# A hybrid decoder step on one core: operations set a stretch of work behind their loads, a sum of exponentials for each engine, and one chunk of the last head moved ahead

## The chip, the cores and the metric

The kernel runs on one core of a Trainium2 chip. The metric is the device time of one execution in microseconds (us); a shorter time is better. The core has five engines that run side by side, each in its own order: TensorE (PE in the profile; PEld is its loading of weights), VectorE (DVE), ScalarE (ACT), GpSimd (POOL) and SyncE (SP, which here only issues transfers). Transfers between memory and the core's buffers run on 16 DMA engines. An engine that meets an operation whose operand isn't there stands until it is, with everything behind it.

## The reference, cut to what matters

One layer is computed for a prompt of 2048 positions and for 8 decoded rows (one position each, with 512 cached positions in pages of 128):

```python
h = rms_norm(x, g_norm);  p = h @ w_in                  # 1024 -> 3592 columns
q, k, v, fz, za, u, gv, zc = split(p)
q, k = rms_norm per head;  logf = log_sigmoid(fz + b_f) # 8 heads of 64
c = cumsum(logf)
attn = softmax(q.k * SCALE + c_t - c_s, causal) @ v     # forgetting attention
mix  = tril(w_s) @ rms_norm(gv) + b_s                   # in chunks of 128 positions
y = x + concat(attn * silu(za), u * mix * silu(zc)) @ w_out
```

Outputs are y for prompt and decoded rows, and k, v, logf and the normalised gv.

## The kernel before, in words

All large products are made of two or three products of a high and a low part in a 32-bit format that TensorE takes in one pass; `split` (line 222) makes the parts: ACT, DVE or POOL writes the high part, DVE (L230) the rest. `split_weights` does the same with a factor.

There are three phases on TensorE.

Projections (lines 1083 to 1167): eight column groups of w_in, over 16 tiles of 128 positions for the first five groups, then over two of the four chunks of 512 positions for u, zc and za (`NCP = 2`; the other two chunks are left for later). After the first group, `gates` (497) makes log sigmoid and its running sum: `turn` transposes four blocks in a row on TensorE (L518, L160), ACT copies (L520), DVE scans (L521), and the split rows go to DRAM.

Attention (1170 to 1204): for each of 8 heads, `maxima` (842) computes the score products once to find each query's extreme (products into a `tp` bank, a DVE reduction at L861); `shifts` (868) turns four of them into rows by a TensorE transpose of `mx` (L876, L881) and sends them to DRAM. `values` (902) then computes for chunk c of 512 queries and key tile kt of 128 keys the scores (two products into one of two `sc` banks), the exponential on ACT (L926) into `p`, a sum of `p` into `acc` on POOL, every fourth on DVE (L933, L936), and, eight key tiles at a time, the products with the values (`av`). `add_up` and `done` transpose `acc` and send the reciprocal sums to DRAM (`rT`). `load_queries` (820) fetches the next chunk's queries and shifts three key tiles before the chunk ends. The maxima run 0.6 of a head ahead.

Filler: while attention runs, TensorE gets other products between its key tiles. `fill(ns)` (783) adds to a debt, which is paid in steps of three products (648 ns); `FILL` is the share of the attention's own time that is added. The generator `fillers` (775) gives first the 24 pieces of the projections that were left (12 column groups, two chunks each; `fill_weights` at 729 loads and splits 128 columns on POOL, L736 to L739), then loads w_out (`load_out_weights`, 992), then gives the output tiles.

Output (`out_tiles`, 1053): for each of 16 tiles of 128 positions `out_inputs` (1006) loads attention rows, gates, mixed rows and reciprocal sums (`az`, `m`, `r`), multiplies them on POOL and DVE (L1018, L1019) and splits them on ACT and DVE; `out_products` (1026) makes 48 products and adds x (L1038). What the attention phase leaves of this runs behind it.

The decoded rows run along: `decode_qk` and `decode_scores` during the projections, `decode_gate` at head 1 and `decode_attention` from head 2, `decode_out` and `out_sample` among the output tiles.

What sets the order: TensorE's instructions run as the program is written. The code keeps a clock of its own, `Pe.clock`, to which each product adds an expected time. `later(ns, fn)` puts `fn` off until that clock has moved on by `ns`, and `pump` runs what is due; `yield ns` in the decode generators does the same. The other engines' instructions and the DMA issues are ordered at build time by the Tile framework, from the order in the program, what is ready and which buffers are free. Buffers come from pools: 16 of 8 KB a partition (`s8`), 11 of 4 KB (`s4`), 3 for raw weights, `WK` of 2 KB (`s2`).

Of the kernel before, what the change touches and what calls it, by code (L numbers as in the profile page):

```python
# [36 lines left out]
FILL = 0.41  # L37
FILL7 = 0.42
LAG = 6400.0
AVB = 8  # L40
WK = 10
# [4 lines left out]
QCS = (0, 1, 2, 3)  # L46
DSUM = 4
# [4 lines left out]
DSTART = 2  # L52
OAHEAD = 2
# [17 lines left out]
def hymba_step(ctx, tc, x_prompt, x_sample, cache_k, cache_v, cache_logf, page_table, g_norm, w_in,  # L71
# [425 lines left out]
    def gates():  # L497
# [16 lines left out]
        def turn():  # L514
            for b in range(4):
                pt = bank("tp")
                for j in range(4):
                    transpose(pt[:NH, j * P:(j + 1) * P], lf3[:, 4 * b + j], ident)  # L518
                lT, cs = s2(t="lT")[:NH], s2(t="cs")[:NH]
                nc.scalar.copy(lT, pt[:NH])  # L520
                nc.vector.tensor_tensor_scan(cs, ones8, lT, 0.0 if b == 0 else last[:, b - 1:b],  # L521
                                             op0=ALU.mult, op1=ALU.add)
                nc.vector.tensor_copy(last[:, b:b + 1], cs[:, 511:512])
# [24 lines left out]
    def decode_gate():  # L548

        gvp = from_ps(OGV)  # L550
        gvn, _ = scaled(gvp, norm_factors(gvp, NG, P, rows=B), NG, P, rows=B)
        gvb = s2(t="gvb")[:B]
        nc.sync.dma_start(gvb, g_v[0].partition_broadcast(B))
        nc.vector.tensor_tensor(gvn, gvn, gvb, op=ALU.mult)
        nc.sync.dma_start(gvs_out, gvn)
        m2 = s2(t="m2")[:B]
# [4 lines left out]
        nc.vector.scalar_tensor_tensor(m2, m2, 0.5, from_ps(OU), op0=ALU.mult, op1=ALU.mult)  # L561
        nc.vector.tensor_tensor(m2, m2, silu2(from_ps(OZC)), op=ALU.mult)
        nc.sync.dma_start(am_s[:, 512:], m2)
        nc.sync.dma_start(z_s, silu2(from_ps(OZA)))
# [64 lines left out]
    def decode_attention():  # L629
# [5 lines left out]
        yield 5000  # L635
# [13 lines left out]
        own = small(8)[:BH]  # L649
        nc.sync.dma_start(own[:, 0:1], tiny[0].rearrange("b (h o) -> (b h) o", o=1))  # L650
        nc.sync.dma_start(own[:, 1:2], tiny[1].rearrange("b (h o) -> (b h) o", o=1))
# [3 lines left out]
        nc.vector.tensor_tensor(own[:, 2:3], own[:, 2:3], own[:, 0:1], op=ALU.min)  # L655
        nc.scalar.activation(lg, lg, AF.Exp, bias=own[:, 2:3], scale=-1.0, accum_out=own[:, 3:4])
        nc.scalar.activation(own[:, 4:5], own[:, 0:1], AF.Exp, bias=own[:, 2:3], scale=-1.0)
        nc.vector.tensor_tensor(own[:, 5:6], own[:, 3:4], own[:, 4:5], op=ALU.add)
# [26 lines left out]
    def decode_out():  # L685
# [6 lines left out]
        nc.vector.tensor_tensor(a2.rearrange("p (n d) -> p n d", n=NH),  # L692
                                from_ps(OV).rearrange("p (n d) -> p n d", n=NH),
                                prs.unsqueeze(2).to_broadcast([B, NH, HD]), op=ALU.mult)
        o4, ob, zb = s8(t="o4")[:B], s2(t="ob")[:B], s2(t="zb")[:B]
        nc.sync.dma_start(o4.rearrange("b (g n d) -> b g n d", g=NPG, n=NH),
                          o_s.rearrange("b g (n x) -> b g n x", n=NH)[:, :, :, :HD])
        nc.vector.tensor_reduce(ob, o4.rearrange("b (g f) -> b f g", g=NPG), axis=AX.X, op=ALU.add)
        nc.sync.dma_start(zb, z_s)
        nc.vector.tensor_tensor(a2, a2, ob, op=ALU.add)  # L700
        nc.vector.scalar_tensor_tensor(a2, a2, 0.5, zb, op0=ALU.mult, op1=ALU.mult)
        return am

    def out_sample(am):
# [7 lines left out]
        xys = s4(t="xys")[:B]  # L712
        nc.sync.dma_start(xys, xs)
# [15 lines left out]
    def fill_weights(o):  # L729
# [172 lines left out]
    def values(hd):  # L902

        h = hd["h"]
        for at, c in enumerate(QCS):
# [333 lines left out]
```

## Time and profile before

| | before |
|---|---|
| median of 3 runs | 1393.12 us (1387.74 to 1395.0) |
| the profiled execution | 1391.17 us, span 1389.5 us |
| TensorE busy | 1313.2 us, 95% of the span |
| VectorE, ScalarE, GpSimd busy | 704.3, 436.2, 548.6 us |
| TensorE's mean granted clock | 0.978 |
| moved by DMA | 174.71 MB, mean 126 GB/s |

The span runs from the first to the last instruction. Busy is the time in which at least one instruction of the engine ran; matmuls overlap and their ends are modelled, so a busy TensorE need not be at its peak. The granted clock is the share of full speed that TensorE was given; it is 1 or 0.5 at any moment. By the tile view the last filler product ran at 1180.8 us, and the output products follow it.

### The profile page before, as it was taken

Reading aid. Unit: us, or ns where it says so; the run is one execution under the profiler, and the core shown is the slowest. Engines: PE = TensorE matmul, PEld = TensorE weight load, DVE = VectorE, ACT = ScalarE, POOL = GpSimd, SP = SyncE. Lnnn points to the kernel's source line nnn. Section 1 sums busy time; section 2 is a strip of 40 time slices with the busy share of each in tenths; the row PEclk is TensorE's granted clock in tenths of the full one; section 3 lists DMA queues with packets and bytes.
Section 4 is the critical chain, followed back from the end, with each engine's and each line's share of the span. In section 5 each row is a group of like instructions: output and inputs, shape, how many; then the busy total and the mean of one; then the engine's idle time right before and its main releaser. Section 6 shows DMA issues by size and latency. Waiting matters only on the chain. (4 is left out here: it accounts for less than half of the span.)

```text
span 1389.5 us, 19601 instructions
## 1 busy us (share of the span) xinstructions
PE 1313.2 (95%) x6544; PEld 1012.4 (73%) x6544; DVE 704.3 (51%) x1376; ACT 436.2 (31%) x797; POOL 548.6 (39%) x647
## 2 busy tenths in 40 slices
PE   6998999999999999999998999999999959969998
PEld 5998999999887777766665665666656635748877
DVE  4446454535677544366655554555565663335131
ACT  5442222323122111034444443444444444211010
POOL 3113343323224555336654554646564444211010
PEclk9999999999999999999999999999999989989999
DMA  6553344545115565564325343455451253677521
GB/s 220 177 129 92 82 137 118 161 133 146 50 42 141 170 184 169 148 151 106 82 54 142 78 126 97 127 137 137 123 131 49 73 169 106 170 186 199 157 67 61
DMA packets 180791, 174.71 MB, mean 126 GB/s; under 512 B 39146, under 2 KB 141994, under 8 KB 179122
## 3 DMA queue, kind: packets, MB, share of 16 engines
q1 hardware_dynamic: 176802, 164.69, 44.3%
q10 hardware_dynamic: 3488, 8.39, 1.6%
q8 instruction: 52, 0.85, 0.3%
q14 instruction: 49, 0.40, 0.1%
q0 software_dynamic: 400, 0.38, 0.1%
HBM read 117.34 MB, written 56.08 MB: 125 GB/s over the span
## 5 line engine op out<-in xcount | busy, mean ns | idle before, releaser
L926 ACT ACTIVATE p<-sc,zero 128x512 f32<-128x512 f32 (+1 forms) x320 | 196.3, 623 | 186.1 <-PE sc L156 171.7
L936 POOL TENSOR_TENSOR acc<-acc,p 128x512 f32<-128x512 f32 (+2 forms) x176 | 202.5, 1150 | 130.5 <-ACT p L926 70.9
L861 DVE TENSOR_REDUCE mn<-tp 128x1 f32<-128x384 f32 (+6 forms) x320 | 189.5, 605 | 123.0 <-PE tp L156 120.5
L156 PE MATMUL acc<-wh,hh 128*128 128x384 f32 (+2 forms) x640 | 229.4, 358 | 0.4 <-ACT wh L235 0.4
L156 PE MATMUL acc<-wl,hh 128*128 128x384 f32 (+2 forms) x640 | 223.6, 349 | 1.2 <-DVE wl L238 1.2
L156 PE MATMUL acc<-wh,hl 128*128 128x384 f32 (+2 forms) x640 | 223.3, 349 | 0.6 <-DVE hl L230 0.6
L156 PE MATMUL sc<-q,k 128*128 128x512 f32 (+7 forms) x640 | 208.3, 402 | 5.5 <-ACT p L926 5.3
L156 PEld LDWEIGHTS sc<-q,k 128*128 128x128 f32 (+1 forms) x640 | 117.1, 197 | 28.0 <-ACT p L926 12.1
L156 PE MATMUL av<-p,vst 128*64 128x512 f32 (+3 forms) x640 | 135.9, 545 | 0.0
L156 PE MATMUL tp<-k,q 66*128 66x384 f32 (+6 forms) x320 | 124.2, 400 | 9.2 <-DVE mn L861 6.2
L156 PEld LDWEIGHTS acc<-wh,hh 128*128 128x128 f32 x640 | 121.4, 190 | 7.6 <-ACT wh L235 0.7
L156 PEld LDWEIGHTS acc<-wl,hh 128*128 128x128 f32 x640 | 121.4, 190 | 6.7 <-DVE wl L238 2.1
L156 PEld LDWEIGHTS acc<-wh,hl 128*128 128x128 f32 x640 | 121.0, 189 | 6.4 <-DVE hl L230 1.2
L218 POOL TENSOR_SCALAR sm<-sm 128x6 f32<-128x6 f32 (+3 forms) x84 | 20.9, 249 | 245.5 <-DVE sm L371 182.6
L156 PE MATMUL av<-wo,am 128*128 128x512 f32 x384 | 95.4, 407 | 10.8 <-DVE xy L1038 10.8
L156 PEld LDWEIGHTS av<-p,vst 128*64 128x64 f32 x640 | 47.9, 138 | 68.0 <-issue 59.3
L156 PEld LDWEIGHTS av<-wo,am 128*128 128x128 f32 x384 | 75.9, 198 | 28.0 <-DVE xy L1038 11.6
L156 PE MATMUL sc<-wo,am 128*128 128x512 f32 x384 | 90.6, 391 | 3.9 <-DVE xy L1038 2.8
L219 POOL TENSOR_TENSOR sm<-sm,mhalf 128x6 f32<-128x6 f32 (+3 forms) x84 | 89.0, 1060 | 6.7
L156 PEld LDWEIGHTS sc<-wo,am 128*128 128x128 f32 x384 | 71.8, 188 | 20.1 <-DVE xy L1038 3.3
L156 PEld LDWEIGHTS tp<-k,q 66*128 66x128 f32 x320 | 62.7, 196 | 32.3 <-DVE mn L861 8.9
L156 PE MATMUL fl<-hh,fh 128*128 128x512 f32 x192 | 81.7, 426 | 1.1 <-DVE sz L472 1.0
(209 smaller groups left out, 2021.9 us busy)
## 6 DMA issues: line engine op xcount, KB each, us to landing
raw<-in_w_in_dram SPq DMA_DIRECT2D x40, 256.0 KB
kb<-in_cache_k_dram SPq DMA_DIRECT2D x32, 256.0 KB
k<-qk_hi SPq DMA_DIRECT2D x16, 512.0 KB
q<-qk_hi SPq DMA_DIRECT2D x64, 128.0 KB
vb<-in_cache_v_dram SPq DMA_DIRECT2D x32, 256.0 KB
xy<-in_x_prompt_dram SPq DMA_DIRECT2D x16, 512.0 KB
out_dram<-xy ACTq DMA_DIRECT2D x15, 512.0 KB
xp<-in_x_prompt_dram SPq DMA_DIRECT2D x12, 512.0 KB
```

The lines of the kernel that those rows point to most:

```text
L156: nc.tensor.matmul(out, lhsT, rhs, start=start, stop=stop)
L218: nc.gpsimd.tensor_scalar(r, ss, inv_n, EPS, op0=ALU.mult, op1=ALU.add)
L219: nc.gpsimd.tensor_tensor(r, r, mhalf[:rows, :n], op=ALU.pow)
L861: nc.vector.tensor_reduce(part[:, i % 4, n:n + 1], sp, axis=AX.X, op=ALU.min)
L926: nc.scalar.activation(p[:, n0:], sp[:, n0:], AF.Exp, bias=zero1, scale=-1.0)
L936: eng.tensor_tensor(acc[:, n0:], acc[:, n0:], p[:, n0:], op=ALU.add)
```

## The change

- `gates`: the four blocks are no longer turned in one go; each block's split comes `GLAG` (2500 ns) after its transposes and then starts the next block.
- `shifts`: the transpose of the maxima comes 3000 ns behind them (`SLAG`) instead of 1500.
- `decode_gate` and `decode_attention`: loads first, then a `yield` of 6000 or 8000 ns, then the operations on them; both start at head 1 (`DSTART`), one behind the other.
- `fill_weights`: its two halves are split 7000 and 14000 ns behind their loads (`FLAG`); the filler waits for them. The first filler weights are loaded in the projection phase.
- `load_out_weights`: eight loads 1500 ns apart (`WOSTEP`), each split 7000 ns behind its load (`WOLAG`).
- `out_inputs`: loads m, z, a, r and now x, and the operations come 11000 ns later (`OLAG`); three tiles ahead instead of two (`OAHEAD`). `decode_out` is a generator with its loads ahead of its operations, and starts at tile 8 instead of 9.
- `values`: DVE sums every fourth exponential, and the one of key tile 2, into a tile of its own, `accd`; POOL sums the others into `acc`, the last diagonal one too, and adds `accd` to it once a chunk. `WK` grows by one for `accd`.
- The chunks of attention are one list, `UNITS`, in which (7, 0) stands ahead of (6, 3). `FILL` is 0.50 instead of 0.41, and 0.95 instead of 0.42 for the last three chunks.

```diff
-FILL = 0.41
-FILL7 = 0.42
+FILL = 0.50
+FILL7 = 0.95
+FLAG = 7000.0
+WOLAG = 7000.0
+WOSTEP = 1500.0
+OLAG = 11000.0
+SLAG = 3000.0
-WK = 10
+WK = 11
-QCS = (0, 1, 2, 3)
-DSUM = 4
+UNITS = [(h, c) for h in range(6) for c in range(4)] + [(6, 0), (6, 1), (6, 2), (7, 0), (6, 3), (7, 1), (7, 2), (7, 3)]
-DSTART = 2
-OAHEAD = 2
+DSTART = 1
+DGATE = 6000.0
+OAHEAD = 3
...
-        def turn():
-            for b in range(4):
...
+        def turn(b=0):
...
+            def parts():
                 ch, cl = s2(F32R, "ch")[:NH], s2(F32R, "cl")[:NH]
                 split(ch, cl, cs, "act")
                 for r, t in enumerate((ch, cl)):
                     nc.sync.dma_start(kx[:, r, b * 512:(b + 1) * 512], t.bitcast(F32))
+                if b < 3:
+                    turn(b + 1)
+            later(GLAG, parts)
...
     def decode_gate():
 
+        gvb = s2(t="gvb")[:B]
         gvp = from_ps(OGV)
-        gvn, _ = scaled(gvp, norm_factors(gvp, NG, P, rows=B), NG, P, rows=B)
-        gvb = s2(t="gvb")[:B]
         nc.sync.dma_start(gvb, g_v[0].partition_broadcast(B))
+        yield DGATE
+        r = norm_factors(gvp, NG, P, rows=B)
+        yield DGATE
+        gvn, _ = scaled(gvp, r, NG, P, rows=B)
...
+        u_, zc_ = from_ps(OU), from_ps(OZC)
...
+        yield DGATE
+        nc.vector.scalar_tensor_tensor(m2, m2, 0.5, u_, op0=ALU.mult, op1=ALU.mult)
...
+        za_ = from_ps(OZA)
+        yield DGATE
+        nc.sync.dma_start(z_s, silu2(za_))
...
-        yield 5000
+        own = small(8)[:BH]
+        nc.sync.dma_start(own[:, 0:1], tiny[0].rearrange("b (h o) -> (b h) o", o=1))
+        nc.sync.dma_start(own[:, 1:2], tiny[1].rearrange("b (h o) -> (b h) o", o=1))
+        yield 8000
...
+            got.extend((hi[:, k], lo[:, k]) for k in range(4 * half, 4 * half + 4))
+        for half in range(2):
+            raw = raw2().rearrange("p (k f) -> p k f", k=4)
+            nc.sync.dma_start(raw, w[half * 512:(half + 1) * 512, o:o + P].rearrange("(k p) f -> p k f", p=P))
+            later(FLAG * (1 + half), lambda half=half, raw=raw: halves(half, raw))
+        return got
...
-        later(1500, turn)
+        later(SLAG, turn)
...
+            if kt == 0 or kt == 2 and c:
+                p0 = p
+            elif kt == 1:
+                if n0:
+                    nc.gpsimd.memset(p[:, :n0], 0.0)
+                    n0 = 0
+                nc.gpsimd.tensor_tensor(acc, p0, p, op=ALU.add)
+            elif kt == 3 and c:
+                nc.vector.tensor_tensor(accd, p0, p, op=ALU.add)
+            elif kt % 4 == 3 and kt < 4 * c:
+                nc.vector.tensor_tensor(accd, accd, p, op=ALU.add)
+            else:
+                nc.gpsimd.tensor_tensor(acc[:, n0:], acc[:, n0:], p[:, n0:], op=ALU.add)
+                if kt == 4 * c + 1:
+                    nc.gpsimd.tensor_tensor(acc, acc, accd, op=ALU.add)
...
+            raw = raw2()
+            nc.sync.dma_start(raw, wo[k * P:(k + 1) * P, f * 512:(f + 1) * 512])
+
+            def parts():
+                split(hi, lo, raw, WOENG[n % len(WOENG)])
+                wo_hl[k, f] = hi, lo
+            later(WOLAG, parts)
+        for n, k in enumerate(KORDER):
+            later(n * WOSTEP, lambda n=n, k=k: load(n, k))
...
+        nc.sync.dma_start(xy, x[t0:t0 + P])
+        got = {}
+
+        def parts():
+            nc.gpsimd.tensor_tensor(z4, z4, r4, op=ALU.mult)
+            am = s8(F32R, "am")
+            hi, lo = (am[:, r * D:(r + 1) * D].rearrange("p (k t) -> p k t", k=KT) for r in range(2))
+            split(hi[:, 4:], lo[:, 4:], m4, "act")
+            nc.vector.scalar_tensor_tensor(a4, a4, 0.5, z4, op0=ALU.mult, op1=ALU.mult)
+            split(hi[:, :4], lo[:, :4], a4, "act")
+            got.update(hi=hi, lo=lo, xy=xy)
+        later(OLAG, parts)
+        return got
...
+            while i not in ins or not ins[i] or len(wo_hl) < 2 * KT:
                 prepare(i)
+                if last_phase[0]:
+                    Pe.waiting.pop(0)[2]()
+                else:
+                    yield -1
...
+                        fw = s8(F32R, "fw")
+                        first.append(fill_weights(OZA, (fw[:, :D], fw[:, D:])))
                         Pe.side = Pe.clock + SSTART
...
+    accd = s2(t="accd")
...
+    for at, (h, c) in enumerate(UNITS):
...
+        dose = FILL if at < len(UNITS) - 3 else FILL7
```

More of the change, by code (lines that the diff above doesn't have):

```diff
@@ L512, in step @@
                 later(3000, turn)
-        def turn():
-            for b in range(4):
[L516 to L523, printed above, removed]
+        def turn(b=0):
+            pt = bank("tp")
+            for j in range(4):
+                transpose(pt[:NH, j * P:(j + 1) * P], lf3[:, 4 * b + j], ident)
+            lT, cs = s2(t="lT")[:NH], s2(t="cs")[:NH]
+            nc.scalar.copy(lT, pt[:NH])
+            nc.vector.tensor_tensor_scan(cs, ones8, lT, 0.0 if b == 0 else last[:, b - 1:b],
+                                         op0=ALU.mult, op1=ALU.add)
+            nc.vector.tensor_copy(last[:, b:b + 1], cs[:, 511:512])
+            def parts():
                 ch, cl = s2(F32R, "ch")[:NH], s2(F32R, "cl")[:NH]
@@ L726, in out_sample, with fill_weights, halves @@
         nc.sync.dma_start(ys, xys)
-    def fill_weights(o):
-        hi, lo = (s4(F32R, t).rearrange("p (k f) -> p k f", k=KT) for t in ("fh", "fl"))
-        for half in range(2):
-            raw = raw2().rearrange("p (k f) -> p k f", k=4)
-            nc.sync.dma_start(raw, w[half * 512:(half + 1) * 512, o:o + P].rearrange("(k p) f -> p k f", p=P))
+    def fill_weights(o, pair=None):
+        hi, lo = (t.rearrange("p (k f) -> p k f", k=KT) for t in pair or (s4(F32R, "fh"), s4(F32R, "fl")))
+        got = []
+        def halves(half, raw):
             for k in range(4):
@@ L753, in filler @@
             unit = units.pop()
+            while len(unit) < KT:
+                yield -1
             for cp in range(NCP, 4):
@@ L762, in filler @@
                 yield 0
+        while min(len(unit) for unit in units) < KT:
+            yield -1
         for cp in range(NCP, 4):
@@ L992, in load_out_weights, with load @@
     def load_out_weights(f):
-        for n, k in enumerate(KORDER):
+        tiles = []
+        def load(n, k):
             if n % 2 == 0:
-                t = s8(F32R, "wo")
+                tiles.append(s8(F32R, "wo"))
+            t = tiles[-1]
             hi, lo = (t[:, (2 * (n % 2) + r) * 512:(2 * (n % 2) + r + 1) * 512] for r in range(2))
@@ L999, in load_out_weights @@
             nc.sync.dma_start(raw, wo[k * P:(k + 1) * P, f * 512:(f + 1) * 512])
-            split(hi, lo, raw, WOENG[n % len(WOENG)])
-            wo_hl[k, f] = hi, lo
+            def parts():
[4 more added lines that the diff above has]
+            later(n * WOSTEP, lambda n=n, k=k: load(n, k))
     def rows_of(t, t0):
@@ L1038, in out_products @@
             nc.vector.tensor_tensor(xy[:, fs], xy[:, fs], po, op=ALU.add)
+            yield 0
             if i == NT - 1:
@@ L1066, in out_tiles @@
                 pump(all_=True)
-                am = decode_out()
-            if i == 10:
-                gs = out_sample(am)
-                next(gs)
-            yield from out_products(i, *ins.pop(i), ("sc", "av") if last_phase[0] else ("fl", "fl"))
-            if i == 10:
+                gs = decode_out()
+            if gs is not None and i < 12:
                 next(gs, None)
+            yield from out_products(i, **ins.pop(i), tags=("sc", "av") if last_phase[0] else ("fl", "fl"))
     mgen = all_maxima()
@@ L1181, in hymba_step @@
         pump()
-    qload[0, QCS[0]] = load_queries(0, QCS[0])
-    for h in range(NH):
-        if h + 1 < NH:
+    qload[UNITS[0]] = load_queries(*UNITS[0])
+    vdone = 0.0
+    for at, (h, c) in enumerate(UNITS):
+        if c == 0 and h < NH - 1:
             heads[h + 1] = load_keys(h + 1)
-        vdone = 0.0
-        if h == DSTART - 1:
-            decode_gate()
-        if h == DSTART:
-            Pe.decode, Pe.steps = Pe.clock, decode_attention()
-        for c in values(heads[h]):
-            vdone += c
-            fill(c * (FILL if h < NH - 1 else FILL7))
+        if (h, c) == (DSTART, 0):
+            Pe.decode, Pe.steps = Pe.clock, chain(decode_gate(), decode_attention())
+        dose = FILL if at < len(UNITS) - 3 else FILL7
+        for v in values(at):
+            vdone += v
+            fill(v * dose)
             pump()
-            while mdone[0] / MT < min(h + vdone / VT + AHEAD, NH):
+            while mdone[0] / MT < min(vdone / VT + AHEAD, NH):
                 m = next(mgen, None)
```

179 lines of the change are left out of this document (76 added, 103 removed).

## The prediction

> **What bounds the kernel now.** I read the page's head first, then a table of stages (busy time and granted clock of each engine in stretches I cut at the visible gaps), then TensorE's waits, then the order of time around each gap.
>
> ```profile
> span 1389.5 us, 19601 instructions
> PE 1313.2 (95%) x6544; PEld 1012.4 (73%) x6544; DVE 704.3 (51%) x1376; ACT 436.2 (31%) x797; POOL 548.6 (39%) x647
> ```
> TensorE (PE) is the bound: 76.3 us idle in the whole span, and no other engine above 51%. So the change can gain only idle time of TensorE and the half clock that follows it. By stage (columns: stretch, its length, busy time of PE, its weight loads, DVE, ACT and POOL, then the granted clock, the DMA share and GB/s):
>
> ```profile
> 0.00:25.00 25.00, 13.98 (x72) 12.16 (x73) 13.06 (x25) 12.56 (x21) 9.39 (x25) 1.00 0.76 255
> 125.00:150.00 25.00, 21.00 (x115) 19.68 (x113) 16.06 (x29) 8.14 (x15) 6.28 (x8) 0.86 0.30 72
> 575.00:610.00 35.00, 33.04 (x145) 22.93 (x145) 22.16 (x42) 5.53 (x12) 15.02 (x27) 0.90 0.32 88
> 675.00:700.00 25.00, 22.82 (x99) 15.03 (x98) 18.11 (x31) 11.27 (x20) 13.18 (x18) 0.86 0.36 96
> 750.00:775.00 25.00, 19.75 (x90) 13.49 (x91) 13.21 (x29) 9.86 (x19) 6.08 (x6) 0.86 0.50 91
> 840.00:865.00 25.00, 23.06 (x102) 14.02 (x99) 10.83 (x23) 7.89 (x15) 9.28 (x11) 0.86 0.20 49
> 865.00:1115.00 250.00, 245.21 (x1234) 156.39 (x1234) 144.32 (x276) 113.59 (x204) 144.81 (x152) 1.00 0.42 112
> 1115.00:1150.00 35.00, 20.64 (x86) 11.53 (x86) 23.82 (x35) 16.17 (x30) 13.01 (x10) 0.85 0.55 164
> 1180.00:1260.00 80.00, 64.59 (x255) 51.29 (x256) 26.24 (x41) 13.57 (x23) 15.03 (x12) 0.89 0.77 190
> ```
> Idle is length less PE busy. The first stretch (11.0 us of start) is not touched by the change, nor is the end after 1260. Where the clock stands below 1.00, a part ran at half: 0.14 of 25 us is 3.5 us lost, beside the idle time. Seven stretches matter: 125 (4.0 idle + 3.5 clock), 575 (2.0 + 3.5), 675 (2.2 + 3.5), 750 (5.3 + 3.5), 840 (1.9 + 3.5), 1115 (14.4, and of 35 × 0.15 = 5.3 about half, since idle time lies in it: 2.6) and 1180 (15.4, and of 80 × 0.11 = 8.8 about 5.8). TensorE's waits (total, times, longest) say who is late:
>
> ```profile
> PE tp L160 <- DVE mx L876: 17.0, 9, 9.8
> PE av L156 <- DVE xy L1038: 10.8, 2, 6.2
> PE tp L156 <- DVE mn L861: 6.2, 3, 4.2
> PE sc L156 <- ACT p L926: 5.3, 6, 2.8
> PE tp L160 <- ACT lT L520: 4.0, 3, 2.0
> ```
> Nearly all name VectorE (DVE). Why it is late stands in the order of time (start, length, instruction, in brackets the idle time before and what ended it):
>
> ```profile
> 134.66 0.60 PE L160 MATMUL tp<-ident,lf 128*8 128x128 f32 x4 [1.77 <-ACT lT L520]
> 594.88 0.27 PE L160 MATMUL tp<-ident,mx 128*8 128x128 f32 x1 [1.26 <-DVE mx L876]
> 684.26 0.48 PE L156 MATMUL tp<-k,q 66*128 66x480 f32 x1 [1.66 <-DVE mn L861]
> 686.16 0.72 ACT L539 ACTIVATE th<-ps,zero 8x512 f32<-8x512 f32 x1 [2.77 <-DMA ps<-p_s]
> 760.28 0.15 DVE L652 TENSOR_TENSOR sm<-sm 64x1 f32<-64x1 f32 x1 [4.90 <-DMA sm<-tiny]
> 761.03 0.77 PE L156 MATMUL tp<-k,q 66*128 66x480 f32 x1 [4.16 <-DVE mn L861]
> 844.02 1.43 POOL L736 TENSOR_SCALAR raw<-raw,gT 128x128 f32<-128x128 f32 x4 [4.63 <-DMA raw<-in_w_in_dram]
> 846.18 1.35 DVE L936 TENSOR_TENSOR acc<-acc,p 128x128 f32<-128x128 f32 x1 [7.58 <-POOL acc L936]
> 848.88 0.30 PE L160 MATMUL tp<-ident,acc 128*128 128x128 f32 x1 [1.94 <-DVE mn L861]
> 1129.43 0.62 ACT L225 CAST wo<-raw 128x512 fp32r<-128x512 f32 x1 [5.23 <-DMA raw<-in_w_out_dram]
> 1144.75 0.38 PE L160 MATMUL tp<-ident,mx 128*8 128x128 f32 x1 [9.77 <-DVE mx L876]
> 1245.23 1.26 POOL L1018 TENSOR_TENSOR az<-az,r 128x512 f32<-128x512 f32 x1 [9.99 <-DMA m<-mT]
> 1249.24 0.80 PE L156 MATMUL av<-wo,am 128*128 128x512 f32 x1 [6.25 <-DVE xy L1038]
> ```
> One pattern: an engine stands at an operation whose load has not landed, and what TensorE needs is queued behind it. At 760 a 0.15 us DVE addition waits 4.90 us for a tiny load, and the maxima behind it hold PE for 4.16. At 844 POOL waits for a weight load, DVE waits for POOL's accumulator, PE for DVE.
>
> **The change, part by part**, each taken as a share of the loss above.
>
> *Gate rows (125).* The four blocks' transposes stood back to back; now 2.5 us of projection products lie between them on PE, and the copy and scan they wait for fit into that. Nothing is added. Takes 7.0 of 7.5.
>
> *Maxima shifts, 3000 instead of 1500 ns.* PE's transpose of mx comes 1.5 us later. Of the 17.0 us, 9.8 belong to stage 1115; the other eight waits are 7.2 us, 0.9 each, less than 1.5. With them goes the half clock at 575, where the first filler weights are also split earlier. I take 4.0 of 5.5 there and 4.5 of the other 6.0 (the one at 594.88 lies in 575). What is late next is the query load, which reads the shifts: it is issued three key tiles before its unit; for the moved chunk (7, 0) I followed the code's own bookkeeping of PE time, by which the load comes 8 us after the shift, so it is not late.
>
> *Decode gate (675).* Loads go out 6000 ns of PE work ahead, at four places. Takes 4.5 of 5.7. *Decode attention (750).* The tiny load goes 8000 ns ahead of the block instead of into its middle. Takes 8.0 of 8.8. Both begin one head earlier, with the same instructions.
>
> *An accumulator for each engine (840).* DVE's additions no longer wait for POOL's, only for the exponential; a merge on POOL is added.
>
> ```profile
> DVE acc L936 <- POOL acc L936: 58.3, 37, 7.6
> POOL acc L936 <- DVE acc L936: 32.9, 20, 7.4
> L936 POOL TENSOR_TENSOR acc<-acc,p 128x512 f32<-128x512 f32 x120 | 155.0, 1291 | 119.3 <-ACT p L926 62.8 <-DVE acc L936 32.9 <-DVE mn L861 5.4
> L936 POOL TENSOR_TENSOR acc<-acc,p 128x256 f32<-128x256 f32 x32 | 23.4, 731 | 2.8 <-ACT p L926 1.0
> L936 DVE TENSOR_TENSOR acc<-acc,p 128x512 f32<-128x512 f32 x48 | 34.3, 715 | 31.3 <-POOL acc L936 26.4 <-ACT p L926 4.6
> L936 DVE TENSOR_TENSOR acc<-acc,p 128x128 f32<-128x128 f32 x32 | 13.8, 431 | 32.2 <-POOL acc L936 31.8 <-ACT p L926 0.2
> ```
> POOL gives 24 additions (key tile 2) to DVE's sum and gains 24 merges, the same 1.29 us each; the 32 diagonal ones of 128 columns go from DVE (0.43) to POOL. That size is not in the trace on POOL: between nothing and 0.73 (256 columns), and the line from 1291 over 731 gives 0.45, which I take; so POOL +14 us over some 570, from 58% busy (144.8 of 250) to 61%, hidden by that room; without the room it would cost those 14 (23 at 0.73). DVE loses those 32 and the 58.3 us of standing. Takes 4.5 of 5.4: POOL may still wait for raw, but DVE no longer stands behind it.
>
> *Filler and output weights (1115).* A head is 17408 columns × 0.422 ns for the maxima (7.35 us) and four times that for the values (29.4). The filler's 24 pieces of 24 × 0.216 us are 124 us: at 0.41 that is 303 us of head work, more than the 294 there are, at 0.50 it is 249, so it ends in head 6 and the wo loads move from the last head to there. The 16 loads are spaced by 1500 ns, the splits put 7000 behind. But engines take operations in the order in which they become ready, not as the code stands:
>
> ```profile
> 1080.48 0.35 SPq L999 DMA_DIRECT2D raw<-in_w_out_dram  x1
> 1122.96 1.50 SPq L999 DMA_DIRECT2D raw<-in_w_out_dram  x3
> ```
> The first wo load went 40 us before the others, as soon as one of three raw buffers came free. So the lag binds TensorE's steps and what takes a new buffer in turn, and the splits perhaps not. Bounds 0 and 17.0; I take 8, the middle, since the tile inputs that shared the queue then (DMA 0.55) come later.
>
> *Output tiles (1180).* In this stretch 0.77 of the DMA engines' time is taken while several tiles' inputs arrive at once. Now three tiles ahead are asked for (two before), m first and x with them, and the first four can start before the longest unit of head 6, since (7, 0) goes ahead of (6, 3). Per tile the inputs are 1.5 MB; asked for some 30 us earlier they come at a lower rate. Same instructions; one more working buffer, which accd takes. Bounds 0 and 21.2; I take 13.
>
> *What is new.* Between the filler's end and the first tile PE has only values for about 19 us of its work (8 × 1500 + 7000), 20 key tiles. The exponential takes 0.69 us (below), PE's two score products 2 × 512 × 0.422 = 0.43 by the same bookkeeping, in runs of eight: 5.5 against 3.5, so 2.0 us late a run, or 0.6 with two banks (1.4) ahead; over two and a half runs 1.5 to 5. I take 3.5.
>
> ```profile
> L926 ACT ACTIVATE p<-sc,zero 128x512 f32<-128x512 f32 x224 | 152.5, 688 | 149.1 <-PE sc L156 138.9 <-POOL p L931 3.8 <-POOL acc L936 1.9
> ```
> Sum: 7.0 + 4.0 + 4.5 + 4.5 + 8.0 + 4.5 + 8 + 13 = 53.5, less 3.5: 50 us. The profiled execution took 1391.2 us (span 1389.5 and 1.7 around it), 1.9 under the median of 1393.1: 1341.2 in its terms, **1342** as forecast.
>
> **Rivals.**
> *A. The lags do nothing off TensorE.* For it: the load at 1080. Then only PE's own steps and the split accumulator count: 7.0 + 8.5 + 4.5, 6 of the decode (where new buffers hold the order), less 3.5: 22 us, 1369. Against it: the decode loads sat in the middle of their block in the trace, so their place does follow the code.
> *B. The last two stages stay bound by transfers.* 0.77 busy at 190 GB/s is near what the trace reaches at all (255 at the start). Then 8 and 13 go: 1363.
> *C. All of it goes.* 7.5 + 5.5 + 6.0 + 5.7 + 8.8 + 5.4 + 17.0 + 21.2 = 77, and nothing new: 1314.
> *D. The half clock stays.* It may not come from the short gaps, and three of the seven half clocks counted lie behind gaps of 1.3 to 1.9 us (575, 675, 840): 3.5 × 3 = 10.5 then remain, 1352. Against it, two finer stretches:
>
> ```profile
> 844.00:849.20 5.20, 3.26 (x16) 2.41 (x15) 3.02 (x4) 2.07 (x3) 4.63 (x7) 1.00 0.00 0
> 849.20:856.00 6.80, 6.80 (x23) 4.49 (x22) 4.29 (x13) 1.67 (x4) 1.63 (x2) 0.50 0.28 78
> ```
> Half clock for 6.8 us follows at once on 1.94 us of idle time. The Trainium skill, "TensorE: Matmul & The Clock Gate", What's actually happening, speaks for D: it asks for a whole idle window of about 3.4 us before the clock halves. The trace is against that rule at 849, where 3.26 of the 5.2 us before were busy.
> *E. Slower: POOL's merges.* Place: the merge at the second diagonal tile of 24 units, which waits for DVE's last sum, with two POOL additions and the transposes of acc behind it, these 5 us after the unit. If each merge waited as long as the longest such wait (7.4), PE would stand 2.4 us and lose 3.4 of clock each time: 24 × 5.8 = 139, and with the 50 gained 1480. It breaks even at 2.1 us a unit, 5 + 2.1 = 7.1 of wait without the clock. Against it: 32.9 us over 20 waits is 1.6 on average. The Trainium skill, "GPSIMD Engine Reference", 4.1 Engine selection, speaks for E: elementwise work belongs on VectorE, being about twice as slow on GpSimd; by the rows here 1291 stands against 715 ns.
> *F. No change:* the waits only change their names, each gap reappears before the next late operand; 1391.
>
> **How the numbers follow.** Chances: forecast 0.40, A and B together 0.25, C 0.14, D 0.07, E 0.07, F 0.07. The time is the forecast's. A and B (to 1369), C (1314) and D lie within 1312 to 1378, the ends a few us beyond them; outside are E and F. Half a per cent, about what a measurement here can tell, is 7 us: faster than 1386 are forecast, A, B, C and D, 0.86, and 0.01 of F; same 0.06; slower 0.07.
>
> **What would show it.** No wait of PE on lT, none over 1 us on mx; no clock of 0.5 near 135, 760 and 849; DVE's wait on POOL's acc from 58 us to under 15; fl products ending by 1100; PE's idle time from 76 to about 40 us. If DVE still waits for xy or wo loads as long, A or B is right; if tp<-ident,acc waits for POOL by tens of us, E.

## The result, and the profile after

The changed kernel took 1382.4 us (median of 12 runs, 1379.0 to 1389.8) against 1390.2 us of the kernel before beside it (12 runs, 1385.8 to 1398.4). The ratio is 0.9945, with a 95% interval from 0.992 to 0.997: 7.7 us faster. 50 us were forecast, and the range (1312 to 1378) does not hold the time. Its profiled execution took 1381.7 us.

The head of the page, after:

```profile
span 1379.9 us, 19555 instructions
...
PE 1311.9 (95%) x6544; PEld 1007.3 (73%) x6544; DVE 704.4 (51%) x1344; ACT 434.3 (31%) x797; POOL 572.0 (41%) x679
```

TensorE's idle time is 68.0 us (1379.9 less 1311.9), where it was 76.3 and about 40 had been forecast. To see where the time went I counted, in both traces, the work that TensorE has done by each moment (columns of each product, at least 256, at 0.422 ns), and compared the moments at which both kernels have done the same work. Negative is a lead of the changed kernel, in us:

```
work done    before at   changed
      120        152.3      -6.4
      600        684.3      -9.4
      720        837.9     -20.8
      760        890.8     -27.5
      880       1029.9     -27.1
      960       1126.2     -14.2
     1000       1190.0     -19.0
     1040       1252.0     -31.0
     1080       1295.5      -9.6
     1164       1384.7      -9.6
```

So up to 1003 us of its time the changed kernel is 27 us ahead, much as forecast; in the two last stages it gives 17.5 of them back. The stages of the kernel after (columns as in the prediction: stretch, length, busy time of PE, weight loads, DVE, ACT, POOL, granted clock, DMA share, GB/s):

```profile
120.00:145.00 25.00, 25.00 (x157) 24.20 (x156) 18.15 (x36) 10.05 (x19) 8.89 (x10) 1.00 0.36 87
...
665.00:690.00 25.00, 25.00 (x133) 17.16 (x130) 16.59 (x27) 11.96 (x23) 19.32 (x25) 1.00 0.53 142
...
1030.00:1100.00 70.00, 62.21 (x289) 39.24 (x288) 43.14 (x78) 31.15 (x59) 27.65 (x26) 0.93 0.39 109
1100.00:1150.00 50.00, 42.36 (x169) 24.11 (x167) 27.27 (x40) 23.20 (x43) 31.80 (x27) 0.79 0.43 118
...
1220.00:1290.00 70.00, 52.69 (x209) 41.59 (x208) 22.45 (x32) 5.99 (x10) 6.39 (x5) 0.90 0.57 156
```

The first two rows are the places at 125 and 675 of the prediction, shifted by the lead: full clock, and no idle time. The last three are where it is lost. The same last stretch before the change:

```profile
1220.00:1290.00 70.00, 59.22 (x236) 47.84 (x235) 26.40 (x35) 7.34 (x12) 7.68 (x6) 0.88 0.77 200
```

Before, TensorE did more there while more was moved (200 GB/s). Now TensorE stands 17.3 of 70 us with the DMA engines 0.57 busy. TensorE's waits of the kernel after, over the whole span (total, times, longest):

```profile
PE av L161 <- DVE xy L1081: 11.6, 4, 9.0
PE tp L165 <- DVE sm L989: 10.0, 4, 6.8
...
PE tp L161 <- ACT mt L914: 4.9, 2, 4.6
PE sc L161 <- ACT am L230: 4.8, 1, 4.8
...
PE tp L165 <- DVE mx L907: 2.3, 3, 1.3
```

Of the 17.0 us on mx 2.3 are left, and lT is gone. In their place stand waits on the sum of a row's exponentials (sm), on mt, on am, and still on xy. The longest, in order of time (start, length, instruction, idle time before and what ended it):

```profile
1250.78 0.34 ACTq L1086 DMA_DIRECT2D out_dram<-xy  x1
1250.80 5.78 PE L161 MATMUL av<-wo,am 128*128 128x512 f32 x24 [1.55 <-DVE xy L1081]
...
1257.83 5.74 PE L161 MATMUL sc<-wo,am 128*128 128x512 f32 x24 [1.25 <-DVE xy L1081]
1259.37 0.36 SPq L1057 DMA_DIRECT2D xy<-in_x_prompt_dram  x1
...
1261.11 0.55 SPq L1052 DMA_DIRECT2D az<-zT  x1
...
1269.94 1.26 POOL L1061 TENSOR_TENSOR az<-az,r 128x512 f32<-128x512 f32 x1 [20.52 <-DMA az<-zT]
1271.23 0.69 DVE L1065 SCALAR_TENSOR_TENSOR az<-az 128x512 f32<-128x512 f32 x1 [13.46 <-POOL az L1061]
1271.84 0.68 DVE L1081 TENSOR_TENSOR xy<-xy,av 128x512 f32<-128x512 f32 x1
...
1272.58 3.78 PE L161 MATMUL av<-wo,am 128*128 128x512 f32 x8 [9.01 <-DVE xy L1081]
```

Read it backwards. TensorE wants the bank `av` again. The 24 products that filled it ended at 1256.6, but VectorE adds them to xy only at 1271.84, because it stood 13.46 us at `az` of a later tile. That waited for POOL, POOL for a load of z, and the load of z was issued only at 1261.11: it lay in SyncE's queue behind a load of x, which got its buffer 8.6 us after the store of 1250.78 had been issued. SyncE's own waits between 1150 and 1300 us show that stand as the longest of its row:

```profile
SPq L1057 <- DMA out_dram<-xy: 12.4, 2, 9.9
```

TensorE did not lack its own operands; it waited for a sum queued behind somebody else's input. Two more such places, at the end of the filler and in the last chunks:

```profile
1095.40 0.62 ACT L230 CAST wo<-raw 128x512 fp32r<-128x512 f32 x1 [5.99 <-DMA raw<-in_w_out_dram]
...
1097.52 0.25 ACT L914 COPY mt<-tp 8x128 f32<-8x128 f32 x1
...
1097.82 0.71 PE L161 MATMUL tp<-k,q 66*128 66x416 f32 x1 [4.58 <-ACT mt L914]
...
1136.79 0.69 DVE L1065 SCALAR_TENSOR_TENSOR az<-az 128x512 f32<-128x512 f32 x1 [5.83 <-POOL az L1061]
...
1138.02 0.68 DVE L988 TENSOR_REDUCE sm<-tp 128x4 f32<-128x512 f32 x1
...
1139.59 1.26 POOL L1061 TENSOR_TENSOR az<-az,r 128x512 f32<-128x512 f32 x1 [2.83 <-issue]
...
1142.09 0.17 DVE L989 RECIPROCAL sm<-sm 128x4 f32<-128x4 f32 x1
1142.32 0.08 PEld L165 LDWEIGHTS tp<-ident,sm 128*4 128x4 f32 x1 [7.23 <-DVE sm L989]
```

At 1095 ScalarE stands 5.99 us at the split of an output weight, and the copy `mt` that frees a bank is behind it. At 1136.79 VectorE has stood 5.83 us at the inputs of a tile; it then works through the inputs of two tiles with POOL, and a reciprocal of 0.17 us, ready since 1138.7, comes last. VectorE's wait at a tile's inputs, before and after:

```profile
DVE az L1019 <- POOL az L1018: 38.0, 12, 6.1
```

```profile
DVE az L1065 <- POOL az L1061: 71.3, 13, 13.5
```

It nearly doubled. What the change put ahead is not only loads, but also the operations that stand for them.

### The profile page after: what moved, and what is told of

It is laid out like the page before. It is cut to its first block, busy times and chain, and to the rows that moved or that the text cites. A ratio compares the mean times of both kernels' runs of the same rounds, so it can differ in the third digit from the quotient of the medians.

```text
span 1379.9 us, 19555 instructions
## 1 busy us (share of the span) xinstructions
PE 1311.9 (95%) x6544; PEld 1007.3 (73%) x6544; DVE 704.4 (51%) x1344; ACT 434.3 (31%) x797; POOL 572.0 (41%) x679
## 5 line engine op out<-in xcount | busy, mean ns | idle before, releaser
L965 POOL TENSOR_TENSOR acc<-acc,p 128x512 f32<-128x512 f32 (+3 forms) x184 | 192.4, 1046 | 126.9 <-ACT p L952 116.6
L161 PE MATMUL av<-p,vst 128*64 128x512 f32 (+3 forms) x640 | 139.4, 556 | 0.2 <-ACT p L952 0.2
L161 PEld LDWEIGHTS sc<-q,k 128*128 128x128 f32 (+1 forms) x640 | 117.3, 198 | 29.4 <-ACT p L952 12.6
L161 PE MATMUL tp<-k,q 66*128 66x384 f32 (+6 forms) x320 | 120.7, 392 | 6.3 <-ACT mt L914 4.9
L161 PE MATMUL av<-wo,am 128*128 128x512 f32 x336 | 81.6, 400 | 11.6 <-DVE xy L1081 11.6
L161 PE MATMUL sc<-wo,am 128*128 128x512 f32 x336 | 80.4, 396 | 6.0 <-ACT am L230 4.8
L161 PEld LDWEIGHTS av<-wo,am 128*128 128x128 f32 x336 | 64.7, 194 | 27.0 <-DVE xy L1081 13.3
L161 PE MATMUL acc<-hh,wh 128*128 128x512 f32 x192 | 75.8, 395 | 4.2 <-DVE s L365 4.2
L161 PEld LDWEIGHTS sc<-wo,am 128*128 128x128 f32 x336 | 64.0, 191 | 20.4 <-ACT am L230 5.2
```

Source lines behind the costliest of these rows:

```text
L161: nc.tensor.matmul(out, lhsT, rhs, start=start, stop=stop)
L965: nc.gpsimd.tensor_tensor(acc[:, n0:], acc[:, n0:], p[:, n0:], op=ALU.add)
```

## The experiments

Each comparison ran the kernel before beside the others on the same chip (medians 1390.6 to 1392.8 us). "Saved" is one less the ratio, times 1391 us; the changed kernel saves 7.7 by this (4.2 to 11.1), and the interval of the others is 2.5 to 6 us to either side. Where two ratios are compared, "give or take" is the root of the sum of the squares of their half intervals.

### Which half of the change is at fault?

The theory: the early terms are real, and the new parts of the two last stages bring waits of their own. Rival: those stages are bound by transfers, and whatever comes earlier waits there. One run has the early parts alone:

```diff
-FILL = 0.50, FILL7 = 0.95, (7, 0) ahead of (6, 3)
+FILL = 0.41, FILL7 = 0.42, chunks in natural order
-load_out_weights, out_inputs, out_products, out_tiles, decode_out as changed
+the same functions as before the change
```

> Only the parts that work before 900 us: gate rows by turns, maxima shifts at 3000, the decode's loads ahead, an accumulator for each engine, the filler's first weights early. Filler share, order of the units, output weights and output tiles stand as before the change. Theory 1 (the early terms are real, and the new parts of the two last stages bring waits of their own that eat them): the lead of 27 us that the changed kernel has at 880 us of TensorE work stays to the end, 1390 - 27 = 1363, and DVE xy and mx waits of the last 300 us stay as before the change. Theory 2 (the last two stages are bound by their transfers, so whatever comes earlier waits there): 1380 to 1390.

The other has the late parts alone:

```diff
-SLAG, decode_gate, decode_attention, the sums in values, fill_weights as changed
+the same as before the change
 gates (turn, GLAG): as changed
```

> Only the late parts: filler share 0.50, order of the units, output weights spaced and put behind their loads, output tiles three ahead with x among their inputs, the sample rows at tile 8. Gate rows, shifts, decode, accumulator and the filler's first weights stand as before the change. Theory 1: the late parts cost what the changed kernel loses behind 880 us of work, 27.1 - 9.6 = 17.5 us: 1408, slower than before. Theory 2: the same as before within 5 us, 1385 to 1395. If it is faster than before by over 7 us, the late parts are not where the gain went, and the early terms are.

Measured: the early parts alone took 1374.3 us (ratio 0.9894, 0.985 to 0.9938; 14.7 saved), the late parts alone 1400.9 (1.0069, 1.0042 to 1.0095; 9.6 lost). All four expected times are missed (1363 and 1380 to 1390; 1408 and 1385 to 1395). e2 kept one early part, other than its expectation says: its gate rows are the changed ones, TensorE has no wait on lT and no idle time between 120 and 150 us there, and it leads by some 6 us at 120 us of work. So the late parts themselves cost more than the 9.6. The rival falls: with the filler's old share the early parts have a lead of 14.9 at 880 us of work, not 27, but all of it lasts to the end (14.7 saved), and the late half makes the kernel slower.

### Which late part?

```diff
 e3: the changed kernel with
-OAHEAD = 3; out_inputs, out_products, out_tiles, decode_out as changed
+OAHEAD = 2; the same as before the change
```

> The changed kernel with the output stage of before: inputs two tiles ahead in the old order and worked on where they are asked for, x loaded with the products, sample rows at tiles 9 and 10. Theory 1, narrowed to the output stage (SyncE's queue stands for buffers there, since x is held from the inputs on and the z and a loads lie behind it): the 21.4 us that the changed kernel loses between 1040 and 1080 us of its work come back but for the 6 that the stage lost before, 1382 - 15 = 1367. Rival (it is the early filler and output weights that cost, at 1040 to 1150 us): no change or slower, 1380 to 1395.

```diff
 e4: the changed kernel with
-FILL = 0.50, FILL7 = 0.95, (7, 0) ahead of (6, 3)
+FILL = 0.41, FILL7 = 0.42, chunks in natural order
```

> The changed kernel with the filler share of before (0.41, 0.42) and the units in natural order, so the filler ends in the last head again; output weights and output tiles as changed. Theory 1, narrowed to the output stage: its waits stay but come later, 1375 to 1385. Rival (the early end of the filler, values without filler and the moved chunk cost the 13 us lost between 920 and 960 us of work): 1382 - 13 = 1369 or less.

Measured: with the old output stage 1369.5 us (0.9852, 0.9812 to 0.9891; 20.6 saved, 12.9 more than the changed kernel, give or take 6.5). The last stretch in e3, to be read against the 52.69 us above:

```profile
1220.00:1290.00 70.00, 58.63 (x241) 46.82 (x240) 24.92 (x33) 6.04 (x11) 6.28 (x5) 0.90 0.60 168
```

With the old filler it took 1392.2 us (1.002, 0.9996 to 1.0043): 10.4 us worse than the changed kernel (give or take 4.8), a miss of both expectations. So the new output stage costs some 13 us, and the larger filler share, with the order of the units, is worth 10. It earns them elsewhere than expected: in e4 the lead at 880 us of work is 16.0, not 27.1, since at 697 and 747 us of time two waits (2.6 us on mx, 1.5 on acc) have a half clock behind them. The changed kernel has no such wait on mx, and full clock behind its own wait of 1.5 us on acc.

### What in the output stage?

Three of its steps were taken back one at a time, and once together:

```diff
 e5: x loaded, and its buffer taken, in out_products again, not in out_inputs
 e6: -OAHEAD = 3  +OAHEAD = 2
 e7: decode_out at tile 9, out_sample at tile 10, as before the change
 e9: e5, e6 and e7 together
```

> The changed kernel with one thing undone: x is loaded with a tile's products again, and takes its buffer there, not among the inputs. The old output stage as a whole won 12.9 us (1369.5). If x among the inputs is the cause (two of the eleven large buffers held per tile asked for, SyncE's queue standing for one with z and a loads behind it): at least 8 of these come back, 1374 or less, and the longest wait of TensorE on xy in the last stage (9.0) goes. If it is the third tile ahead or the sample rows at tile 8: 1378 to 1386.

> The changed kernel with inputs asked for two tiles ahead, not three; x still among them. If the number of large buffers in flight is the cause, from either end, this wins as much as x with the products: 1374 or less. If x's place alone decides: 1378 to 1386. If three ahead was worth something, as forecast: over 1386.

> The changed kernel with the sample rows' loads at tile 9 and their products at tile 10, in the old order of their operations. Theory of the buffers: one or two of the eleven large buffers (am, xys) are taken one tile later, a few us at most, 1378 to 1384. Rival (the sample rows, their 3.8 us reduction on VectorE and their loads ahead of the z loads cost the stage its 13 us): 1374 or less.

> The changed kernel with x loaded with the products, inputs two tiles ahead and the sample rows at tiles 9 and 10: the three single steps that won 8.4, 7.4 and 9.6 us, together. The lags and the order m, z, a of the loads stay. If the three relieve one shortage, they don't add: the old output stage as a whole won 12.9, 1369.5; the lags, worth 5.4 with three tiles ahead, may add to it: 1364 to 1370. If they are three causes of their own, they add to 25: 1357.

Measured: 1374.0, 1375.0, 1372.8 and together 1372.4 us (ratios 0.9868, 0.9890, 0.9847 and 0.9866). Each alone saves 7.6 to 13.6 us more than the changed kernel (give or take 5 to 6), and together they save no more. e5 came out at the edge of its theory, e7 as its rival had it, e6 between two expectations and e9 outside both of its own. Steps that don't add look like one cause, touched from three sides. A shortage of the eleven large buffers (az, xy, and two for the sample rows) would be such a cause, so one was taken away:

```diff
+            if i == 6:
+                held.append(s4(t="held")[:, :8])
+                nc.gpsimd.memset(held[0], 0.0)
...
+        if i == 13:
+            nc.vector.tensor_tensor(xy[:, :8], xy[:, :8], held[0], op=ALU.add)
```

> The changed kernel with one of its eleven large buffers taken away for the output stage: it is filled with zeros at tile 6, and eight of its columns are added to the sum of tile 13, one operation each. If the shortage is of these buffers, one less costs about what each of the three single steps won by giving back one or two: 7 to 10 us, 1389 to 1392. If it is the order of the loads in SyncE's queue or the transfers themselves, and not the number of buffers: the same within 4 us, 1378 to 1386.

Measured: 1374.7 us (0.9887, 0.985 to 0.9923). With a buffer less it is 8 us faster, not slower: the theory of the shortage falls, and the rival's 1378 to 1386 is missed as well. What all these steps change is the order in the engines' queues. The next four asked for bytes, stores and queue:

```diff
 e13: the load of x, and its addition, cut to 128 of 1024 columns (the rest of x is left out of y)
 e14: y stored in two halves, one behind each sum, not in one store
 e15: the same on e3
 e16: -nc.sync.dma_start(xy, x[t0:t0 + P])  +nc.scalar.dma_start(xy, x[t0:t0 + P])
```

> The changed kernel with only 128 of x's 1024 columns loaded and added per output tile (the other seven eighths of x are left out of y, their sums are copied instead). Same buffers held from the same points, same number of loads in the same queue, 7.2 MB less to move, some 38 us of transfers at 190 GB/s. If the last stage is bound by bytes (rival B of the prediction): the 21.4 us lost between 1040 and 1080 us of work shrink to a third, 1361 to 1370. If loads stand in SyncE's queue behind a load whose buffer is not yet stored: at most the stores' landing gets shorter, 1376 to 1384.

> The changed kernel with y stored in halves of 512 columns, the first one 5.2 us of products ahead of the second, in place of one store behind the second; same bytes. If loads stand for a buffer that a y store holds: the last half is 256 KB and lands earlier than 512 KB, each stand of SyncE on out_dram (30 us in 7 now) gets shorter, and 5 to 10 us come back, 1372 to 1377. If bytes bind: no change, 1379 to 1385.

> The changed kernel with the output stage of before (1369.5) and y stored in halves. If buffers held by stores still cost there (SyncE stands 24 us on out_dram in that run): 2 to 6 us, 1363 to 1367. If not: 1368 to 1371.

> The changed kernel with x's loads issued by ScalarE and not by SyncE: same buffers, same bytes, but z and a loads no longer stand behind an x load that has no buffer yet. If the order in SyncE's queue is the cause: the 9.0 us wait of TensorE near 1272 goes, and 8 to 13 us come back, 1369 to 1374, unless ScalarE then stands and the casts of a tile are late. If it is the number of buffers or the bytes: 1378 to 1390.

Measured: e13 1372.4 us (0.9867), between its two expectations. Its longest wait stays, at a low rate. A row of TensorE's waits between 1200 and 1300 us of e13, and the stretch around it:

```profile
PE av L161 <- DVE xy L1082: 7.7, 1, 7.7
```

```profile
1244.00:1260.00 16.00, 8.27 (x37) 6.52 (x35) 3.54 (x8) 1.27 (x3) 1.26 (x1) 0.86 0.35 91
```

With 0.35 of the DMA engines' time taken, full DMA engines don't explain that wait; how much of the 10.8 us that e13 gained is due to them can't be told from its changed order. e14 took 1387.8 us (0.9973): no gain, outside both expectations, and SyncE's waits for stores between 1150 and 1300 us didn't get shorter (32.0 us in 7, against 30.2 in 7); e15 1367.2 (0.9830, 0.9797 to 0.9863), at the edge of its own, and not told apart from e3. e16 took 1376.0 (0.9888, 0.9855 to 0.9922), 7.9 us better than the changed kernel (give or take 5.8) and between its two expectations; the wait of 9.0 us is gone, the longest on xy is 5.4. VectorE's wait for tile inputs between 1200 and 1300 us there, and, for comparison, in the changed kernel:

```profile
DVE az L1065 <- POOL az L1061: 27.9, 7, 6.5
```

```profile
DVE az L1065 <- POOL az L1061: 44.9, 7, 13.5
```

Over all runs, VectorE's longest wait at az in that stretch is 12.9 to 13.7 us in the kernels whose longest wait of TensorE on xy is 7.9 us or more (the changed one, e2, e4, e8, e11, e12, e14), and at most 10.8 in those with 6.2 or less, the kernel before among them. Two don't fit: e9 (6.8 and 8.7) and e10 (12.6 and 5.1). In e13 they are 12.5 and 7.7.

### The order on VectorE

```diff
+            else:          # from tile 4 on
+                nc.scalar.copy(hi[:, 4:], m4)
+                nc.gpsimd.tensor_tensor(lo[:, 4:], m4, hi[:, 4:].bitcast(F32), op=ALU.subtract)
+                nc.gpsimd.tensor_scalar(z4, z4, 0.5, 0.0, op0=ALU.mult, op1=ALU.add)
+                nc.gpsimd.tensor_tensor(a4, a4, z4, op=ALU.mult)
+                nc.scalar.copy(hi[:, :4], a4)
+                nc.gpsimd.tensor_tensor(lo[:, :4], a4, hi[:, :4].bitcast(F32), op=ALU.subtract)
```

> The changed kernel, but from tile 4 on the work on a tile's inputs is taken off VectorE: POOL multiplies (the factor 0.5 in an operation of its own, 128x512) and forms the two low parts, ScalarE casts as now; loads, buffers, queue order and bytes stay. Reading of the order of time near 1272: VectorE stands 13.5 us at a later tile's az, whose z load is late, and the sum xy<-xy,av, ready since 1256.6, is queued behind it; TensorE waits for that sum to free its bank, not for its own operands. If so, the waits of TensorE on xy (12.9 us in 5) fall to under 3 and their half clocks go with them: 1382 - 10 to - 16, 1366 to 1372. If TensorE lacks the operands themselves, the waits only change their name to ACT am or POOL am: 1378 to 1388.

> The same step on the best kernel so far (output stage of before, y in halves, 1367.2): from tile 4 on VectorE has only the sums xy. TensorE's waits on xy behind 1220 us, 9.0 us in 3, and some 5 us of half clock with them are at stake. Theory of VectorE's order: 1355 to 1362. If the operands themselves are late: 1364 to 1370, under the name ACT am or POOL am.

Measured: e17 1372.8 us (0.9862, 0.9825 to 0.9900), 11.5 us more saved than the changed kernel (give or take 6.3), though its loads, buffers and bytes are the same. Its median misses the expected stretch by 0.8 us, and the waits on xy are not under 3 us, as expected; but none on the operands came in their place. TensorE's waits on xy behind 1200 us fell from 12.9 us in 5 to the first row here; the second is VectorE's longest wait in that stretch:

```profile
PE sc L161 <- DVE xy L1089: 5.8, 1, 5.8
```

```profile
DVE am L718 <- POOL am L1074: 18.5, 1, 18.5
```

The one that is left has the same form: VectorE stands at the sample rows' first operation (L718), which was not moved, and four sums xy are queued behind it. e18 took 1364.1 us (0.9808, 0.9768 to 0.9848): the fastest here, some 27 us under the kernel before, but not told apart from e15, and at the edge of the rival's expectation. TensorE's waits between 1220 and 1300 us of e18:

```profile
PE sc L161 <- ACT am L1067: 8.9, 1, 8.9
PE sc L161 <- POOL am L1068: 2.6, 1, 2.6
```

No wait on xy is left, but two for the operands themselves are: in the old output stage VectorE's order hid that the inputs of a tile are late too. So two things hold that stage. In the changed kernel it is the order on VectorE: the waits on xy follow it, and fall by 7.1 us when the work is taken off. The time alone wouldn't show it, since e10, which only shuffled the order, saved nearly as much. Why e10's VectorE can stand as long and hold TensorE less is in its order of time:

```profile
1227.89 0.68 DVE L1081 TENSOR_TENSOR xy<-xy,sc 128x512 f32<-128x512 f32 x1
...
1229.27 0.68 DVE L1081 TENSOR_TENSOR xy<-xy,av 128x512 f32<-128x512 f32 x1
...
1243.19 0.69 DVE L1065 SCALAR_TENSOR_TENSOR az<-az 128x512 f32<-128x512 f32 x1 [12.64 <-POOL az L1061]
...
1246.62 0.79 PE L161 MATMUL sc<-wo,am 128*128 128x512 f32 x1 [5.10 <-DVE xy L1081]
```

Both sums had been made just before VectorE began to stand at 1230.55, so TensorE could fill both banks before it needed one freed, and waited 5.1 us. In the changed kernel the sum of one bank was still to come when the stand of 13.46 us began, and TensorE waited 9.0. So where a stand falls counts beside its length, and the changed kernel's loss is in part a matter of bad luck. Below VectorE's order lie late inputs, which come to light in e18. How the 12.9 us of e3 divide between the two stays open.

### The lags, and two early terms by themselves

```diff
 e8:  -OLAG = 11000.0, WOLAG = 7000.0   +OLAG = 0.0, WOLAG = 0.0
 e11: the sums of values as before the change (one accumulator)
 e12: decode_gate and decode_attention as before the change, one head later
```

> The changed kernel with both lags of the two last stages at nothing: the splits of the output weights and the work on a tile's inputs stand right behind their loads in the code. Rival A of the prediction (a lag does nothing off TensorE): the same within 4 us, 1378 to 1386, with the waits of ACT and POOL on their loads as long as now. If the lags do what they were meant for: slower by the 13 and more that the stages behind 1040 us lost before the change, 1392 or more.

> The changed kernel with the sum of exponentials as before: one accumulator for both engines, every fourth addition on VectorE. Forecast of its term: 4.5 us slower, 1387. By the leads (the changed kernel gains 6.7 us between 720 and 760 us of work, where the late parts alone gain 4.1) 3 to 7 us. Rival E (the merges on POOL cost time): faster, 1378 or less.

> The changed kernel with the decode's gate and attention as before: the loads in the middle of their blocks, one head later. Forecast of the two terms: 4.5 + 8.0 slower, 1395. By the leads between 600 and 720 us of work (the changed kernel gains 11.4 there, and the late parts alone lose 1.0) 12 us of lead, of which the stages behind 1040 us may take some: 1388 to 1395. If under 1386, the lead is lost there whatever it is.

Measured: without the lags 1387.8 us, between the two expectations. The kernel before took 1392.8 beside it, and the ratio, 0.9947 (0.9924 to 0.9969), is that of the changed kernel: the lags of 7 and 11 us are worth nothing that can be measured (0.3 us, give or take 4.7). One accumulator: 1388.2 (0.9984, 0.9952 to 1.0016), 5.4 us worse than the changed kernel, give or take 5.6, with 4.5 forecast: in the expected range, but not told apart from nothing. The old decode: 1398.2 (1.0058, 1.0035 to 1.0082), beyond the 1395 expected at most and 15.7 us worse, give or take 4.8, with 12.5 forecast.

## Why the prediction was wrong, point by point

**Gate rows** (7.0): the lead by 120 us of work is 6.4, and about 6 in e2, which has no other early part. Right. No wait on lT, and no half clock between 15 and 1039 us, so rival D is wrong as well.

**Maxima shifts** (4.0 and 4.5): between 120 and 600 us of work the lead grows by 3.0; between 760 and 880 it doesn't grow (27.5, 27.1). The long waits on mx went, but the second figure was a sum over waits that lie in the other terms' stages.

**Decode gate and attention** (4.5 and 8.0): the lead grows by 11.4 between 600 and 720, and e12 loses 15.7. Right in kind, but the size is not the decode's alone. Counted in the same way, the lead by 720 us of work is 20.8 in the changed kernel, but only 8 to 13 in e1 and e4 (old filler share), e11 (old sum) and e12 (old decode): without any one of the three, most of the growth is missing. (The prediction has both parts begin one head earlier; the gate began at head 1 before as well.)

**An accumulator for each engine** (4.5): e11 loses 5.4, give or take 5.6. The lead grows by 6.7 between 720 and 760, where this term was sought, but by at least as much in e11 without it; what e11 lacks, it lacks before 720. VectorE's wait on acc, 58.3 us before, is gone. Rival E is wrong: the merges took 31.8 us on POOL, as costed, with 1.4 us of idle time before them in all, and an addition of 128 columns took 0.49 us there (0.45 was taken). Both rows of POOL's groups, after:

```profile
L967 POOL TENSOR_TENSOR acc<-acc,accd 128x512 f32<-128x512 f32 x24 | 31.8, 1324 | 1.4
...
L965 POOL TENSOR_TENSOR acc<-acc,p 128x128 f32<-128x128 f32 x32 | 15.5, 486 | 3.1 <-ACT p L952 1.4
```

Together these terms seem to give 27.1 us of lead where 32.5 were forecast. That the two are so close is partly luck: the early parts alone (e1) have 14.9 there, and the rest comes only with the filler's larger share, which the prediction had put into a later stage.

**Filler and output weights** (8, less 3.5 of new cost): between 880 and 1000 us of work the lead falls by 8.1, where a gain of 4.5 was forecast. This is the first step that failed. The filler did end early (at 1091 us), and its share is worth 10.4 us (e4), but in the decode stretch; in its own place the splits of the output weights and the first tiles' inputs now stand in the queues of ScalarE and VectorE while the last chunks need these engines (the rows at 1095 and 1136 to 1142). The marks divide the loss only roughly, since the lead swings from row to row (14.2, 19.0, 31.0). Of the 17.5 us lost behind 880, e3 brings back 12.9, so some 4.6 are left for these parts; the wait at 1142 is not in e3, so it is a cost of the new output stage. No run took the splits away alone. The prediction also misread its row at 1080: it was the second of three early loads of w_out (1031.4, 1080.5, 1082.6), not the first and only one.

**Output tiles** (13, bounds 0 and 21.2): the lead falls by another 9.4, and e3 shows a cost of 12.9 (give or take 6.5) where 13 were to be won. This is the second step that failed, and the larger one. The prediction took the DMA share of 0.77 for the limit, and an earlier request for a cure. But the row it quoted, TensorE's wait on xy, has VectorE in it, and the pattern it had found at 760 and 844 (an engine stands at an operation whose load has not landed, and what TensorE needs is behind it) holds here too: asking for inputs earlier put more of such operations in front of the sums. Its lower bounds of 0 for both stages had no reason; a loss should have been in them.

**Rivals.** Of A (1369), the part on the lags of the last stages is borne out by e8: the sentence "the lag binds TensorE's steps ..., and the splits perhaps not" should have weighed more. Against A, the decode's loads ahead of their operations did their work (e12, which takes back yields and places together). B (1363) came to a time in which those stages give nothing; in fact they took 17.5 us, and not by transfers alone. That a gain in one place is given back in the next, which F held for all gaps, was true of the late half of the change only.

**Chances.** "Faster" held 0.87 and was right, by 7.7 us, hardly more than the 7 that the prediction had set for it; no case held both that the early terms come and that the late ones cost.

## What to carry to other kernels

Before an input is asked for earlier, look at which engine works on it and at what else is queued on that engine: on an engine that takes its instructions in order, an operation that waits for a load blocks the small sum or copy that frees TensorE's bank. A lag in a planner's clock for one engine need not move the operations of the others (e8); moving the waiting operation to an engine whose queue doesn't hold those sums takes the wait away (e17). A lead won early is worth only what the last stage can carry, so cost that stage with a loss among its bounds.

## What the runs showed of the hardware

An addition on VectorE became longer once it no longer took turns with POOL. The two groups of additions into `accd`, after (count, busy us, mean ns):

```profile
L961 DVE TENSOR_TENSOR accd<-p 128x512 f32<-128x512 f32 x24 | 18.9, 786 | 8.4 <-ACT p L952 8.4
L963 DVE TENSOR_TENSOR accd<-accd,p 128x512 f32<-128x512 f32 x24 | 21.5, 894 | 10.1 <-ACT p L952 10.0
```

Before, 48 of the same shape took 715 ns on average. Sorted by what POOL did meanwhile, the 24 of the 48 after that overlap a POOL operation for more than 30% of their time have a median of 0.92 us, the other 24 of 0.69; before, 45 of 48 overlapped POOL for less than that and took 0.69. POOL's own additions went from 1291 to 1325 ns. The Trainium skill, "SBUF — State Buffer", Who interferes with whom, says that a VectorE instruction with two inputs in SBUF contends with a GpSimd instruction that reads SBUF; the trace agrees, at 0.23 us an addition. So the accumulator for each engine paid some 6 us of VectorE time (40.4 against 34.3); whether any of it reached TensorE isn't shown.
